# Gated linear attention: layout of the exponentials, one scaling per head, mask copies and square sums on ScalarE

## The chip, the core and the metric

The kernel runs on one core of one Trainium2 chip. The core has a matrix engine (PE, TensorE, with PEld for its weight loads), a vector engine (DVE, VectorE), a scalar engine (ACT, ScalarE), a general engine (POOL, GpSimd), and a queue engine (SP) from which this kernel sends all its DMA transfers. Each engine takes its instructions in order; they wait for each other through semaphores. Matrix products are written to PSUM, in banks of 128 partitions by 512 float32 numbers; everything else lies in SBUF, 128 partitions wide, and the large arrays in device memory (DRAM).

The metric is the device time of one execution in microseconds (us); lower is better. A profiled execution also has a span, the time from its first to its last instruction.

## The reference

One encoder layer is applied to two sequences of 512 tokens of width 1024. In order: a half-step SwiGLU network and a layer norm, an input projection, two groups of heads side by side (gated linear attention and grouped-query attention), an output projection and a layer norm, a second SwiGLU network and a layer norm, and a gated embedding. All is float32. The part that the change touches is the gated linear attention, four heads with keys of 64 and values of 128, in chunks of 64 tokens and in both directions:

```python
def gla_direction(q, k, v, log_a, inclusive):
    ...
    cum = jnp.cumsum(log_a.reshape(bsz, nc, c, h, dk), axis=2)
    mid = cum[:, :, c // 2 - 1:c // 2]
    last = cum[:, :, c - 1:]
    scores = jnp.einsum('bnihd,bnjhd->bnhij', q * jnp.exp(cum - mid), k * jnp.exp(mid - cum))
    mask = jnp.tril(jnp.ones((c, c), dtype=bool), 0 if inclusive else -1)
    scores = jnp.where(mask, scores, 0.0)
    o_intra = jnp.einsum('bnhij,bnjhe->bnihe', scores, v)
    upd = jnp.einsum('bnjhd,bnjhe->bnhde', k * jnp.exp(last - cum), v)
    ...
    o_inter = jnp.einsum('bnihd,bnhde->bnihe', q * jnp.exp(cum), states)
    return (o_intra + o_inter).reshape(bsz, n, h, dv)
```

The forward direction includes the token itself, the backward one does not. Their sum goes through an RMS norm per head and a gate.

## The kernel before

The whole layer is one program, unrolled. PE's order is written by hand: generators yield a few matrix products at a time, and a `Ticker` weaves the pieces of side work into the main stream of products. The order on the other engines and on SP is made by the framework from program order, dependences and its own time model when the program is built. Buffers come from pools with a fixed number of slots per tag; a tile whose slot is still in use makes its first writer wait for the last reader of the tile before it. PSUM has two pools of four banks: `pm` for the main projections, `pd` for the side work.

`Middle.gla(s)` is the gated linear attention of sequence s. It works on pairs of heads, two pairs for each of the two sequences, so four pairs run one after the other, woven into the products of the output projection (`wout`, products on L715, sums on L1107 and L1109, weights loaded on L149 and split into two parts on L137 and L138). The parts of `gla`:

- `pre(hp)` prepares a pair. L984 loads the log decays `l` (two directions) and L986 loads q and k of both heads of the pair, 128 partitions being two heads of 64, into the other half of the same tile. For each direction `dr` and each half `hf` of the tokens, L998 makes cumulative sums with a constant matrix (four products: a step), L1000 writes two exponentials of them, exp(+) for q and exp(-) for k, into E, and L1002 copies the chunk ends. There are four steps in a pair. L1009, L1011 and L1014 form the decay factors R between chunks. L1016 multiplies q and k by the exponentials into z. In z the two directions of one head lie on partitions 0 to 63 and 64 to 127, whereas in `l`, q, k and E the two heads do. So L1016 goes by direction, head and q or k: eight products of 64 partitions by 512 in a pair. The instructions on L1000 and L1014 are recorded under L176, the line of the helper `expln`.
- `one(h)` loads values gv and gates G of a head (L1024, L1025), transposes k (L1030, copied by L1032), forms the chunk updates (L1037), runs the state recurrence over the eight chunks in both directions (started by the copies L1044 and L1045, then 12 instructions on L1047 and L1049), scales the states (L1050, L1051), forms the scores of both directions (L1059), and writes them through a predicated copy per direction into A (L1061), which was set to zero once (L980).
- `two_a(h)` multiplies scores and states with values and queries into one bank o (L1070, L1073), squares it (L1076), sums the squares (L1078), and scales by norm and gate (L1081). `two_b(h)` transposes that (L1088) and splits it for the output projection (L1089, L1090).

The order around a pair is `one` of both heads, `two_a` of both heads, `pre` of the next pair, and so on. The tiles of `pre`, the states W and the attention's tile PT share one tag with three slots (`m8`). The first pair begins while grouped-query attention (`attn`, with L909 to L952) does its last pieces.

Of the kernel before, what the change touches and what calls it, by code (L numbers as in the profile page):

```python
# [12 lines left out]
AF = mybir.ActivationFunctionType  # L13
ALU = mybir.AluOpType
AX = mybir.AxisListType
# [5 lines left out]
NT = 4  # L21
# [14 lines left out]
            A=(157, 159, 160),  # L36
            seg=((2, 132), (2, 142), (18, 160), (18, 170), (43, 193), (43, 216), (178, 334)),
            b=(4, 3),
# [684 lines left out]
class Middle:  # L723
# [246 lines left out]
    def gla(self, s):  # L970
        nc, L = self.nc, self.L
        f, bw = slice(0, 64), slice(64, 128)
        T = {}

        def pre(hp):
            if hp == 0:
                T["mx"] = L.xp.tile([128, 4, 2, 512], F32R, tag="x", name="mixG")
                self.mix[s, 0] = T["mx"]
                T["A"] = self.vp.tile([128, 2, NT, 128], F32, tag="v", name="A")
                nc.gpsimd.memset(T["A"], 0.0)  # L980
            lq = self.m8("lq", (128, 2, 2, 512))
            l, qk = lq[:, 0].rearrange("p d (t c) -> p d t c", t=NT), lq[:, 1]
            for t in range(NT):
                nc.sync.dma_start(l[:, :, t], self.spill["l", s][t].rearrange("p (d c) -> p d c", d=2)[:, :, hp * 128:(hp + 1) * 128])  # L984
            for i in range(2):
                nc.sync.dma_start(qk[:, i], self.spill["gqk", s][2 * i + hp])  # L986
            yield
            R = [self.sp.tile([128, 8], F32, tag=f"R{e}", name=f"R{e}", bufs=2) for e in range(2)]
            E = self.m8("E", (128, 2, 2, 512))
            z = self.m8("qk1", (128, 2, 2, 512))  # L990
            for e in range(2):
                T["z", 2 * hp + e], T["R", 2 * hp + e] = z[:, e], R[e]
            for dr in range(2):
                sc = self.sp.tile([128, 2, 8], F32, tag="sc", name="sc")
                for hf in range(2):
                    b = L.bank_d().rearrange("p (a n) -> p a n", a=2)
                    for a in range(2):
                        nc.tensor.matmul(b[:, a, :132], l[:, dr, 2 * hf + a], self.L.U[:, dr], start=True, stop=True)  # L998
                    for j, sg in ((0, 1.0), (1, -1.0)):
                        L.expln(E[:, dr, j, hf * 256:(hf + 1) * 256].rearrange("p (a n) -> p a n", a=2),  # L1000
                                             b[:, :, :128], AF.Exp, scale=sg)
                    nc.vector.tensor_copy(  # L1002
                        sc[:, :, hf * 4:hf * 4 + 4].rearrange("p k (a c) -> p a k c", a=2),
                        b[:, :, 128:132].rearrange("p a (k c) -> p a k c", k=2))
                    if hf == 0:
                        yield
                ex = self.sp.tile([128, 7], F32, tag="ex", name="ex")
                if dr == 0:
                    nc.vector.tensor_tensor(ex, sc[:, 1, 0:7], sc[:, 0, 1:8], ALU.add)  # L1009
                else:  # L1010
                    nc.vector.tensor_tensor(ex, sc[:, 1, 1:8], sc[:, 0, 0:7], ALU.add)  # L1011
                for e in range(2):
                    rs, rd = slice(64 * e, 64 * e + 64), slice(64 * dr, 64 * dr + 64)
                    L.expln(R[e][rd, 1 - dr:8 - dr], ex[rs], AF.Exp)  # L1014
                    for i in range(2):
                        nc.vector.tensor_tensor(z[rd, e, i], qk[rs, i], E[rs, dr, i], ALU.mult)  # L1016
                yield

        def one(h):
            cs = slice(h * 128, (h + 1) * 128)  # L1020
            gv = self.m2("gvh", shape=(128, NT, 128))
            G = self.m2("Gh", shape=(128, NT, 128))
            for t in range(NT):
                nc.sync.dma_start(gv[:, t], self.spill["gv", s][t][:, cs])  # L1024
                nc.sync.dma_start(G[:, t], self.spill["G", s][t][:, cs])  # L1025
            q1, k1 = T["z", h][:, 0], T["z", h][:, 1]
            R = T["R", h]
            b = L.bank_d()
            for t in range(NT):
                nc.tensor.transpose(b[:, t * 128:(t + 1) * 128], k1[:, t * 128:(t + 1) * 128], L.ident)  # L1030
            kT = self.m2("kT", shape=(128, NT, 128))
            nc.scalar.activation(kT.rearrange("p a n -> p (a n)"), b, AF.Copy)  # L1032
            yield
            U = [L.bank_d().rearrange("p (c n) -> p c n", c=4) for _ in range(2)]
            for c in range(8):
                rw = slice(64 * (c % 2), 64 * (c % 2) + 64)
                nc.tensor.matmul(U[c % 2][:, c // 2], kT[rw, c // 2], gv[rw, c // 2], start=True, stop=True)  # L1037
            if h % 2 == 0:
                T["W"] = self.m8("W", (128, 2, 8, 128))
            W = T["W"][:, h % 2]  # L1040
            nc.gpsimd.memset(W[f, 0], 0.0)
            nc.gpsimd.memset(W[bw, 7], 0.0)
            up = lambda c, rd: U[c % 2][rd, c // 2]
            nc.scalar.activation(W[f, 1], up(0, f), AF.Copy)  # L1044
            nc.scalar.activation(W[bw, 6], up(7, bw), AF.Copy)  # L1045
            for c in range(1, 7):
                nc.vector.scalar_tensor_tensor(W[f, c + 1], W[f, c], R[f, c:c + 1], up(c, f), ALU.mult, ALU.add)  # L1047
                cb = 7 - c
                nc.vector.scalar_tensor_tensor(W[bw, cb - 1], W[bw, cb], R[bw, cb:cb + 1], up(cb, bw), ALU.mult, ALU.add)  # L1049
            nc.gpsimd.tensor_tensor(W[f, 1:8], W[f, 1:8], R[f, 1:8].unsqueeze(2).to_broadcast([64, 7, 128]), ALU.mult)  # L1050
            nc.gpsimd.tensor_tensor(W[bw, 0:7], W[bw, 0:7], R[bw, 0:7].unsqueeze(2).to_broadcast([64, 7, 128]), ALU.mult)  # L1051
            yield
            A = T["A"][:, h % 2]
            S = [L.bank_d().rearrange("p (a n) -> p a n", a=NT) for _ in range(2)]
            for t in range(NT):
                ts = slice(t * 128, (t + 1) * 128)
                for dr in range(2):
                    rd = slice(64 * dr, 64 * dr + 64)
                    nc.tensor.matmul(S[dr][:, t], k1[rd, ts], q1[rd, ts], start=True, stop=True)  # L1059
            for dr in range(2):  # L1060
                nc.vector.copy_predicated(A, self.L.mask[:, dr].unsqueeze(1).to_broadcast([128, NT, 128]), S[dr])  # L1061
            T["h", h] = gv, G, W, A
            yield

        def two_a(h):
            gv, G, W, A = T["h", h]
            q1 = T["z", h][:, 0]
            o = L.bank_d().rearrange("p (a n) -> p a n", a=4)
            for t in range(NT):
                nc.tensor.matmul(o[:, t], A[:, t], gv[:, t], start=True, stop=False)  # L1070
                for cc in range(2):
                    c = 2 * t + cc
                    nc.tensor.matmul(o[64 * cc:64 * cc + 64, t], q1[:, c * 64:(c + 1) * 64], W[:, c],  # L1073
                                     start=False, stop=True)
            sq = self.m2("osq", shape=(128, NT, 128))
            nc.scalar.activation(sq, o, AF.Square)  # L1076
            ss = L.small(NT, "oss")
            nc.vector.tensor_reduce(ss, sq, AX.X, ALU.add)  # L1078
            r = self.rms(ss, NT, 128.0, GN_EPS, "gn")
            for t in range(NT):  # L1080
                nc.vector.scalar_tensor_tensor(G[:, t], o[:, t], r[:, t:t + 1], G[:, t], ALU.mult, ALU.mult)  # L1081
            yield

        def two_b(h):
            G, mx = T["h", h][1], T["mx"]
            b = L.bank_d()
            for t in range(NT):
                nc.tensor.transpose(b[:, t * 128:(t + 1) * 128], G[:, t], L.ident)  # L1088
            nc.scalar.activation(mx[:, h, 0], b, AF.Identity, scale=self.L.gn)  # L1089
            nc.vector.scalar_tensor_tensor(mx[:, h, 1], b, self.L.gn, mx[:, h, 0].bitcast(F32), ALU.mult, ALU.subtract)  # L1090
            yield

        return pre, one, two_a, two_b

    def wout(self, s, part):
# [348 lines left out]
```

## Time and profile before

| | us |
|---|---|
| Three timed executions | 1960.98, 1953.67, 1956.47 |
| Their median | 1956.47 |
| Profiled execution, device time | 1953.48 |
| Its span | 1951.7 |
| PE busy in it | 1877.6 |
| DVE busy | 1413.1 |
| ACT busy | 873.8 |
| POOL busy | 860.5 |

The granted clock of PE over the span is 0.985 of full speed. Busy times of PE are modelled, since its products overlap. The profile names an instruction by line, engine and operation, then output and input tiles (in its naming `qk` and `qk1` stand for z, `pd` and `pm` for banks), then shapes as partitions by elements. An "x" gives a count. A bracket at the end of a line of the timeline is the time that the engine stood idle before the instruction, and what ended it. A line of who waited for whom gives the total in us, how often, and the longest. In the list of groups, the numbers behind the first bar are busy us in total and mean ns of one, those behind the second the idle us before them. A row of the stretches gives its length and then busy us and number of instructions of PE, PEld, DVE, ACT and POOL, the granted clock, the DMA engines' busy share and GB/s.

### The profile page before, as it was taken

To read this page: it belongs to the slowest core of one execution; us is meant where nothing else is said; L and a number is where in the kernel's file an instruction comes from. 1 tells how busy PE (TensorE), PEld (TensorE's weight loads), DVE (VectorE), ACT (ScalarE), POOL (GpSimd) and SP (SyncE) were. 2 spreads that over 40 slices of the span, in tenths; PEclk is the share of its full clock that TensorE was granted. 3 is DMA by queue.
4 is the path that set the end of the run, shared out by engine and by line. 5 is a ranking of instruction groups with operands and counts; after the bars stand their busy time and mean duration, and the time that the engine had idled before them with its cause. 6 is when DMAs were issued, how large, how long until landed. Compare 5 with 4: busy or idle time off the path is not lost. (4 is left out here: it accounts for less than half of the span.)

```text
span 1951.7 us, 25305 instructions
## 1 busy us (share of the span) xinstructions
PE 1877.6 (96%) x8838; PEld 1535.1 (79%) x8838; DVE 1413.1 (72%) x2143; ACT 873.8 (45%) x1654; POOL 860.5 (44%) x644
## 2 busy tenths in 40 slices
PE   7999999999999898989998898999999999999999
PEld 5788888888888777777876667888888888888787
DVE  7856566666886985788777879556566659895973
ACT  5445544444231355757752437445444442231342
POOL 0665565561550362342233343665565552451243
PEclk9999999999999998999998998999999999999999
DMA  4425443478865224222443231434443479766232
GB/s 180 162 103 173 169 150 144 158 279 343 316 252 195 91 72 156 84 82 92 140 152 87 87 119 55 161 114 158 173 161 141 162 274 338 297 256 247 76 122 84
DMA packets 104959, 322.22 MB, mean 165 GB/s; under 512 B 11008, under 2 KB 38400, under 8 KB 99456
## 3 DMA queue, kind: packets, MB, share of 16 engines
q1 hardware_dynamic: 104832, 320.61, 45.7%
q8 instruction: 70, 1.15, 0.2%
q14 instruction: 57, 0.47, 0.1%
HBM read 218.85 MB, written 101.71 MB: 164 GB/s over the span
## 5 line engine op out<-in xcount | busy, mean ns | idle before, releaser
L138 POOL TENSOR_TENSOR w<-raw,w 128x512 fp32r<-128x512 f32 (+1 forms) x318 | 431.8, 1367 | 750.3 <-ACT w L137 685.6
L137 ACT ACTIVATE w<-raw 128x512 fp32r<-128x512 f32 (+1 forms) x586 | 363.4, 624 | 449.2 <-POOL raw L269 85.8
L269 POOL TENSOR_TENSOR raw<-raw 128x512 f32<-128x512 f32 x240 | 355.9, 1491 | 227.4 <-DVE w L138 155.6
L425 PE MATMUL pm<-X,w 128*128 128x512 f32 x1848 | 434.6, 393 | 10.9 <-ACT X L137 7.8
L425 PEld LDWEIGHTS pm<-X,w 128*128 128x128 f32 x1848 | 347.2, 188 | 89.7 <-ACT X L137 8.6
L138 DVE TENSOR_TENSOR w<-raw,w 128x512 fp32r<-128x512 f32 x268 | 263.2, 990 | 115.5 <-ACT w L137 111.6
L425 PE MATMUL pd<-X,w 128*128 128x512 f32 x1320 | 307.9, 391 | 2.9 <-DVE w L138 2.2
L425 PEld LDWEIGHTS pd<-X,w 128*128 128x128 f32 x1320 | 247.5, 188 | 57.8 <-DVE w L138 3.0
L539 PE MATMUL pm<-w,XB 128*128 128x512 f32 x864 | 198.4, 389 | 0.8 <-DVE Y L523 0.8
L715 PE MATMUL pm<-w,h1T 128*128 128x512 f32 (+1 forms) x768 | 185.6, 384 | 14.0 <-ACT gr L757 9.9
L539 PEld LDWEIGHTS pm<-w,XB 128*128 128x128 f32 x864 | 162.0, 188 | 35.2 <-DVE Y L523 1.7
L138 DVE TENSOR_TENSOR hs<-sg,hs 128x512 fp32r<-128x512 f32 (+1 forms) x182 | 145.4, 818 | 49.6 <-ACT hs L137 48.4
L137 ACT ACTIVATE hs<-sg 128x512 fp32r<-128x512 f32 (+1 forms) x182 | 98.4, 561 | 166.1 <-DVE sg L391 64.8
L715 PEld LDWEIGHTS pm<-w,h1T 128*128 128x128 f32 x768 | 136.3, 195 | 36.5 <-ACT gr L757 10.1
L539 PE MATMUL pd<-w,XB 128*128 128x512 f32 x648 | 148.8, 389 | 0.0
L539 PEld LDWEIGHTS pd<-w,XB 128*128 128x128 f32 x648 | 121.6, 188 | 25.2
L523 DVE TENSOR_TENSOR Y<-Y,pm 128x512 f32<-128x512 f32 x104 | 70.4, 682 | 36.1 <-PE pm L539 36.0
L371 DVE TENSOR_TENSOR sg<-u,pm 128x512 f32<-128x512 f32 x22 | 15.1, 687 | 107.7 <-PE pm L425 107.7
L715 PE MATMUL pm<-w,h3T 128*128 128x512 f32 x384 | 90.6, 393 | 0.0
L715 PEld LDWEIGHTS pm<-w,h3T 128*128 128x128 f32 x384 | 71.2, 188 | 14.7 <-DVE h3T L670 0.2
L660 ACT ACTIVATE pd<-pd,c_lnT 128x512 f32<-128x512 f32 x48 | 36.0, 751 | 92.6 <-PE pd L658 92.6
L523 DVE TENSOR_TENSOR Y<-Y,pd 128x512 f32<-128x512 f32 x88 | 58.7, 678 | 19.3 <-PE pd L539 19.3
(237 smaller groups left out, 2542.1 us busy)
## 6 DMA issues: line engine op xcount, KB each, us to landing
hs<-hs SPq DMA_DIRECT2D x126, 512.0 KB, 2.6
XB<-hs SPq DMA_DIRECT2D x42, 1536.0 KB, 7.0
raw<-in_wgu SPq DMA_DIRECT2D x88, 512.0 KB, 3.4
raw<-in_wd SPq DMA_DIRECT2D x36, 512.0 KB, 7.2
hs_t<-hs SPq DMA_DIRECT2D x56, 256.0 KB, 2.5
XB<-hs_t SPq DMA_DIRECT2D x26, 512.0 KB, 5.1
raw<-in_wout SPq DMA_DIRECT2D x16, 512.0 KB, 3.6
raw<-in_wpg SPq DMA_DIRECT2D x16, 512.0 KB, 3.5
```

The costliest lines, as they stand in the source:

```text
L137: first = nc.scalar.activation(hi, raw, AF.Copy)
L138: (eng or nc.vector).tensor_tensor(lo, raw, hi.bitcast(F32), ALU.subtract)
L269: (sums or self.nc.gpsimd).tensor_tensor(o(), x(), y(), ALU.subtract)
L371: add = lambda o, x, y: nc.vector.tensor_tensor(o, x, y, ALU.add)
L425: nc.tensor.matmul(bank, w[:, a, kt * 128:(kt + 1) * 128], X[k][:, kt, b], start=(k in (0, 1, 4) and kt == 0 and m == 0), stop=(kt == 3 an ...
L523: nc.vector.tensor_tensor(yv, yv, bank, ALU.add)
L539: nc.tensor.matmul(b[t], h[:, a, t * 128:(t + 1) * 128], d[:, c], start=(k in (0, 4, 1) and g == 0 and x == 0), stop=(g == len(H) - 1 and ...
L660: nc.scalar.activation(p, p, AF.Identity, scale=self.lnT[:, c:c + 1], bias=self.lnT[:, c + 8:c + 9])
L715: nc.tensor.matmul(banks[t][:, :width], x[:, i, t * 128:(t + 1) * 128], w[a][:, j], start=(q == 0 and a == 0 and m == 0), stop=(q == nq - ...
```

## The change

Four things change, all in `gla`.

- q and k are no longer loaded beside `l`. Each is loaded twice, straight into z, once for the partitions of each direction: four transfers to 64 partitions in place of two to 128. z's tile is the target, so these loads come after z has its slot.
- The exponentials are written in the layout of z: for each step and each head separately, with 64 partitions, so four in a step in place of two.
- The scaling is one product for a head, over both directions, q and k (128 partitions by 1024), in place, once the second direction's exponentials are there: two in a pair in place of eight.
- In `one`, the predicated copy of the backward direction's scores is replaced by two copies on ACT of the diagonal 64 by 64 blocks, whole; the predicated copy of the forward direction then overwrites what the mask of L1061 selects. In `two_a`, the square over a bank and the sum on DVE are replaced by four squares on ACT, one for each 128 tokens, that give the sum as an accumulator output.

```diff
-            lq = self.m8("lq", (128, 2, 2, 512))
-            l, qk = lq[:, 0].rearrange("p d (t c) -> p d t c", t=NT), lq[:, 1]
+            l = self.m8("l", (128, 2, 2, 512))[:, 0].rearrange("p d (t c) -> p d t c", t=NT)
...
-            for i in range(2):
-                nc.sync.dma_start(qk[:, i], self.spill["gqk", s][2 * i + hp])
             yield
...
             z = self.m8("qk1", (128, 2, 2, 512))
+            for i in range(2):
+                src = self.spill["gqk", s][2 * i + hp].rearrange("(e p) c -> p e c", e=2)
+                for rd in (f, bw):
+                    nc.sync.dma_start(z[rd, :, i], src)
...
-                    for j, sg in ((0, 1.0), (1, -1.0)):
-                        L.expln(E[:, dr, j, hf * 256:(hf + 1) * 256].rearrange("p (a n) -> p a n", a=2),
-                                             b[:, :, :128], AF.Exp, scale=sg)
+                    for e in range(2):
+                        for j, sg in ((0, 1.0), (1, -1.0)):
+                            L.expln(E[64 * dr:64 * dr + 64, e, j, hf * 256:(hf + 1) * 256].rearrange("p (a n) -> p a n", a=2),
+                                    b[64 * e:64 * e + 64, :, :128], AF.Exp, scale=sg)
...
-                    for i in range(2):
-                        nc.vector.tensor_tensor(z[rd, e, i], qk[rs, i], E[rs, dr, i], ALU.mult)
+                    if dr == 1:
+                        nc.vector.tensor_tensor(z[:, e], z[:, e], E[:, e], ALU.mult)
...
-            for dr in range(2):
-                nc.vector.copy_predicated(A, self.L.mask[:, dr].unsqueeze(1).to_broadcast([128, NT, 128]), S[dr])
+            for r in (f, bw):
+                nc.scalar.activation(A[r, :, r], S[1][r, :, r], AF.Copy)
+            nc.vector.copy_predicated(A, self.L.mask[:, 0].unsqueeze(1).to_broadcast([128, NT, 128]), S[0])
...
-            nc.scalar.activation(sq, o, AF.Square)
             ss = L.small(NT, "oss")
-            nc.vector.tensor_reduce(ss, sq, AX.X, ALU.add)
+            for t in range(NT):
+                nc.scalar.activation(sq[:, t], o[:, t], AF.Square, accum_out=ss[:, t:t + 1])
```

## The prediction

> **What bounds the kernel now.** I read the page first, then the chain that ended last over 640 to 1200 us, then the stretch in which the changed lines run, by engine, then who waited for whom in it, then PE, DVE, ACT and SP in order of time. The profiled execution took 1953.48 us, of which the span is 1951.7 us; the median of the three timed runs is 1956.47 us, 3.0 us above it. The sum below is made against 1953.48 and put on the median at the end.
>
> ```profile
> span 1951.7 us, 25305 instructions
> ...
> 997.00:1152.00 155.00, 136.38 (x869) 100.52 (x868) 122.48 (x289) 52.35 (x135) 62.06 (x56) 0.94 0.36 109
> ```
>
> The second row is the stretch of the changed lines, a twelfth of the span; its busy columns are PE, PEld, DVE, ACT, POOL, then the granted clock. PE is busy 136.4 of 155 us. So whatever the change saves on DVE (122.5 us busy, the fullest engine but PE), no more than the 18.6 us in which PE stands still can be won, unless the clock changes.
>
> Gated linear attention runs there in four pairs of heads (two sequences, two pairs each). Within a pair PE goes: four steps of L998 (decay sums), other projections (L715), L1030 of the first head, then heads one and two, then L1070/L1073 of both. Who makes PE wait:
>
> ```profile
> PE pd L1030 <- DVE W L1047: 7.5, 4, 3.1
> ...
> PE pd L1070 <- DVE W L1047: 4.7, 4, 1.3
> ...
> 1012.68 0.63 PE L1030 MATMUL pd<-c_ident,qk 128*128 128x128 f32 x4 [1.02 <-DVE qk L1016]
> ...
> 1045.93 0.63 PE L1030 MATMUL pd<-c_ident,qk 128*128 128x128 f32 x4 [1.62 <-DVE qk L1016]
> ...
> 1083.49 0.63 PE L1030 MATMUL pd<-c_ident,qk 128*128 128x128 f32 x4 [1.04 <-DVE qk L1016]
> ...
> 1117.54 0.63 PE L1030 MATMUL pd<-c_ident,qk 128*128 128x128 f32 x4 [1.79 <-DVE qk L1016]
> ```
>
> The first two rows are the state recurrence (L1047/L1049), which the change leaves alone: 12.2 us that stay. The four timed rows are the first L1030 of each pair, waiting for the scaled q and k of L1016; the number in brackets is PE's wait, 1.02 + 1.62 + 1.04 + 1.79 = 5.47 us. This is the wait that the change addresses. Its start minus its wait is when PE was free: 1011.66, 1044.31, 1082.45, 1115.75.
>
> **The change part by part.** Durations first:
>
> ```profile
> L1016 DVE TENSOR_TENSOR qk<-lq,E 64x512 f32<-64x512 f32 x32 | 25.1, 806 | 0.4
> ...
> L1061 DVE COPY_PREDICATED A<-c_mask,pd 128x512 f32<-128x512 uint32 x16 | 11.6, 726 | 0.4
> ...
> L176 ACT ACTIVATE E<-pd 128x256 f32<-128x256 f32 x32 | 10.7, 375 | 6.1 <-PE pd L998 6.1
> ...
> L1078 DVE TENSOR_REDUCE oss<-osq 128x4 f32<-128x512 f32 x8 | 5.5, 684 | 11.3 <-ACT osq L1076 11.3
> ...
> L1076 ACT ACTIVATE osq<-pd 128x512 f32<-128x512 f32 x8 | 4.8, 598 | 36.3 <-PE pd L1073 36.3
> ...
> L1044 ACT ACTIVATE W<-pd 64x128 f32<-64x128 f32 x8 | 2.2, 270 | 11.2 <-PE pd L1037 11.2
> ...
> L942 ACT ACTIVATE o<-pd 64x256 f32<-64x256 f32 x3 | 1.1, 377 | 1.4 <-PE pd L939 1.4
> ...
> L176 ACT ACTIVATION_READ_ACCUMULATOR P<-pd,nm 128x1 f32 x2 | 0.4, 197 | 0.0
> ...
> L138 DVE TENSOR_TENSOR X<-rest,X 128x1024 fp32r<-128x1024 f32 x6 | 7.3, 1219 | 1.4 <-ACT X L137 1.4
> ```
>
> Scaling: 32 products of 64x512 (25.1 us) become 8 of 128x1024; the nearest row of that size is the last, 1.22 us, so 9.8 us: DVE loses 15.3 us. Exponentials: 32 of 128x256 become 64 of 64x256; a 64x256 read from PSUM takes 377 ns (L942), no less than 128x256, so ACT gains 32 x 0.377 = 12.1 us. Mask: 8 of 16 predicated copies go (5.8 us of DVE), 16 ACT copies of 64 x 4 x 64, 256 elements, come (6.0 us). Square sums: 8 reductions go (5.5 us of DVE); 8 squares of 128x512 become 32 of 128x128 with an accumulator read each. No row shows such a square; L1044 has its 128 elements, so 0.27 + 0.20 = 0.47 us each, 15.0 less 4.8: ACT gains 10.2 us. In sum DVE falls from 122 to about 96 us of the stretch, ACT rises from 52 to about 81. Neither number is the gain: the gain is what leaves PE's waits.
>
> **Step A, first L1030.** What must now be done before it is all four steps of exponentials, then one product of 128x1024. The last exponentials before:
>
> ```profile
> 1007.72 0.63 ACT L176 ACTIVATE E<-pd 128x256 f32<-128x256 f32 x2
> ...
> 1039.54 0.66 ACT L176 ACTIVATE E<-pd 128x256 f32<-128x256 f32 x2 [0.48 <-PE pd L998]
> ...
> 1041.46 0.36 ACT L176 ACTIVATE E<-pd 128x256 f32<-128x256 f32 x1
> ...
> 1079.27 0.63 ACT L176 ACTIVATE E<-pd 128x256 f32<-128x256 f32 x2
> ...
> 1112.94 0.63 ACT L176 ACTIVATE E<-pd 128x256 f32<-128x256 f32 x2
> ```
>
> They end at 1008.35, 1041.82, 1079.90 and 1113.57. Two take 0.66 us, so one more adds 0.28 and a step is 0.56 longer. The first two steps stand apart, with ACT waiting for PE between; the additions of the last two remain, 1.1 us (bounds 0.6 and 2.2). With the product of 1.22 and 0.05 us of handover, k is ready 2.4 us after these ends: 1010.7, 1044.2, 1082.3, 1115.9. PE is free at 1011.66, 1044.31, 1082.45, 1115.75. So PE itself becomes the last to come, and 5.3 of the 5.47 us go. The dependent rest of the pair (L1037, recurrence, second L1030, L1070) moves up with it. What queues behind: on DVE, behind the product that waits for the last exponential, its twin for the second head, then L1090 and L1107 or L1109, which PE needs only a bank or a projection later; on ACT, behind each longer step, weight splits (L137), made up to four pieces ahead, 0.56 us later each. With 2.2 for the additions, 1.1 us later in each pair, some 3.6 us of the 5.3 come back.
>
> **Step B, the recurrence's start.** DVE begins L1047 when ACT's L1045 is done and DVE's queue is clear:
>
> ```profile
> 1048.74 0.27 ACT L1045 ACTIVATE W<-pd 64x128 f32<-64x128 f32 x1
> ...
> 1049.56 0.33 DVE L1047 SCALAR_TENSOR_TENSOR W<-W,R,pd 64x128 f32<-64x128 f32 x1
> ...
> 1120.35 0.27 ACT L1045 ACTIVATE W<-pd 64x128 f32<-64x128 f32 x1
> ...
> 1121.86 0.34 DVE L1047 SCALAR_TENSOR_TENSOR W<-W,R,pd 64x128 f32<-64x128 f32 x1
> ```
>
> DVE was late by 0.55 us in pair 2 and 1.24 in pair 4. Pair 2's goes, as DVE has its products done a microsecond earlier. In pair 4 other work (L1109, L1090, L509) queues on DVE behind the products and moves up less than L1045 does: I count 0.5 of 1.24 (bounds 0 and 1.24). Step B gives 1.0 us.
>
> **Step C, masks and squares.** L1070 waits for the recurrence (row above), not for the masked scores, so the copies hide behind the recurrence, 12 instructions of 0.33 us and more a head; without that cover they would cost two copies and a handover, 0.8 us a head. Four squares in a row take about 4 x 0.39 us (they overlap by 0.1 or less) against 0.60 + 0.69 now: 0.2 us later. That shows only at the last head, where PE has nothing else to put in front: -0.2 us.
>
> **Step D, the loads.** q and k are now loaded twice, four loads of 256 KB for two, into z itself, so they wait for z's buffer; SP sends in order.
>
> ```profile
> 1002.69 1.10 PE L939 MATMUL pd<-PT,V 128*128 128x256 f32 x8
> ...
> 1014.00 1.16 PE L1037 MATMUL pd<-gvh,kT 64*128 64x128 f32 x16
> ...
> L1024 SPq DMA_DIRECT2D gvh<-sp_gv x32: 319/430/1089, 1001.5 to 1116.2; - x32
> ...
> DMA to landing us min/median/max: 1.7/2.3/7.1
> ...
> L986 SPq DMA_DIRECT2D lq<-sp_gqk x8: 430/514/598, 999.9 to 1091.8; - x8
> ...
> DMA to landing us min/median/max: 3.0/4.0/4.5
> ...
> 1034.05 0.44 PE L1073 MATMUL pd<-W,qk 128*64 128x128 f32 x4
> ...
> 1038.81 0.33 SPq L149 DMA_DIRECT2D raw<-in_wout  x1
> ...
> 1072.18 0.44 PE L1073 MATMUL pd<-W,qk 128*64 128x128 f32 x4
> ...
> 1082.63 0.33 SPq L149 DMA_DIRECT2D raw<-in_wout  x1
> ...
> 1105.49 0.44 PE L1073 MATMUL pd<-W,qk 128*64 128x128 f32 x4
> ...
> 1112.58 0.33 SPq L149 DMA_DIRECT2D raw<-in_wout  x1
> ```
>
> z's buffer comes free when the last reader before it ends: for pair 1 attention's last values (L939, 1003.8), for the others the pair before's last L1073 (1034.5, 1072.6, 1105.9). Four issues of 0.51 and a landing of 3.0 to 4.5 us later make 5.0 to 6.5: 1008.8 to 1010.3, 1039.5 to 1041, 1077.6 to 1079.1, 1110.9 to 1112.4. The exponentials now end at about 1009.5, 1042.9, 1081.0 and 1114.7, so the loads hide, by nothing in pair 1 and by 2 us in the others. Behind them on SP wait the heads' gv and G (L1024, L1025) and weights (L149). In pair 1, the tightest, eight issues of 0.43 us behind z's last (1005.9) end at 1009.3 and land 2.3 us later, 1011.6; L1037, which needs them, follows L1030 by 1.3 us and comes at 1013 at the earliest. I take 0; late by a microsecond, pair 1 loses one.
>
> A rule speaks against this step. The Trainium skill, "SBUF — State Buffer", Door 1, says that 64 partitions reach only 8 of the 16 DMA ports, so a transfer to 64 runs at half rate. By its 27.2 GB/s a port the megabyte would take an estimated 4.8 us instead of 2.4, so that the last load lands 2.4 us later than above, 2.4 us too late in pair 1 and 0.4 in the others; the sum would be about 2.6 us. No load of the rows above goes to 64 partitions, so the trace cannot say.
>
> Sum: 5.3 + 1.0 - 0.2 = **6.1 us**, 1953.5 to 1947.4; on the median 1950.4. What follows the stretch, the output projection, is led by PE and moves up whole.
>
> **The rivals.** (1) *The clock.* After some waits PE runs slowly:
>
> ```profile
> 1064.00:1073.00 9.00, 9.00 (x45) 5.69 (x46) 3.99 (x12) 1.34 (x4) 3.37 (x3) 0.62 0.41 118
> 1126.00:1133.00 7.00, 6.28 (x33) 4.63 (x35) 4.61 (x11) 1.14 (x3) 3.35 (x2) 0.54 0.00 0
> ```
>
> Granted 0.62 of 9 us and 0.54 of 7 us, they lose 3.4 + 3.2 = 6.6 us. Shorter waits could spare both: 6.1 + 6.6 = 12.7, so 1944. For it: the second stretch begins at the longest wait, 3.1 us. Against it: most of that wait is recurrence and stays, and the first begins after a wait of 1.3 only. The Trainium skill, "TensorE: Matmul & The Clock Gate", Part 1, lets the clock fall after an idle window of about 3.4 us that runs free of the kernel; by that rule the first stretch would not be there, so the trace agrees in part.
>
> (2) *SP's order*, the slower side. If z's loads come to stand behind the next weight load (L149 at 1038.81, 1082.63, 1112.58, each held by its own wait), q and k land 0.33 + 2.05 + 4.5 us later, and L1030 follows 1.3 us after: 1047.0, 1090.8 and 1120.8 for 1045.9, 1083.5 and 1117.5, so 1.1 + 7.3 + 3.3 = 11.7 us slower: 1968. It decides from a landing after about 1044.7, 1082.2 and 1116.2. For it: SP's order is made anew when the program is built. Against: in the code z's loads stand ahead of the heads' loads, and SP is idle at 1072.6 and 1106.
>
> (3) *ACT takes DVE's place.* If copies, weight splits (L137) and squares get in between the exponentials, the additions are 2.2 us, step B goes, and about 1.5 us are left: 1955. For it: ACT's 29 us more. Against: ACT is a third busy here.
>
> That the change does not do what it says is no case: the instructions follow from the code.
>
> **How the numbers follow.** Forecast 0.45; clock 0.20; ACT 0.22; SP 0.13. The likeliest gives 1950. The clock case with the runs' spread reaches down to 1942, the ACT case and an SP case with one late pair up to 1961; the rest of SP's is left out. About 0.5%, 10 us, can be told from no change here. Faster by more: most of the clock case and a little of the forecast, 0.23. Slower by more: most of SP's, 0.11. Between: 0.66.
>
> **What would show it.** Right: first L1030 of each pair with no wait for L1016's successor, 8 products of about 1.22 us, L1047/L1049 waits as before, ACT near 81 us of the stretch. Wrong: L1030 or the product waiting for a DMA (step D), for an exponential (step A), L1070 for an ACT copy (step C), or the two slow-clock stretches gone or new ones elsewhere.

## The result, and the profile after

The changed kernel takes 1939.28 us (median of four executions, 1938.49 to 1939.72). The kernel before, run beside it, has a median of 1955.07 (four executions, 1949.62 to 1960.98). The ratio of the two is 0.9929 with a 95% interval of 0.9903 to 0.9956, so by the ratio some 14 us or 0.7% are gained. The prediction was 1950.0 with a range of 1942 to 1961: too little gain, and outside the range by 2.7 us.

The profiled execution of the changed kernel took 1939.51 us (span 1937.7), 13.97 less than the one before. All of it lies in the stage of the changed lines. I take that stage from the first decay sum of pair 1 to the last transposes of the last head (L1088 before, L1091 after); those are the bounds of the row of the stretches. First the kernel before:

```profile
1001.31:1148.59 147.28, 128.66 (x827) 94.34 (x827) 116.38 (x275) 48.03 (x126) 59.24 (x53) 0.94 0.35 104
```

The same stage after:

```profile
1002.05:1134.85 132.80, 122.64 (x828) 91.35 (x827) 94.29 (x233) 68.17 (x230) 59.13 (x53) 0.99 0.49 131
```

The stage is 14.5 us shorter. PE does the same work (827 and 828 products). Its busy time falls by 6.0 us, as its granted clock rises from 0.94 to 0.99, and its idle time, length less busy, falls by 8.5 us (18.6 to 10.2). DVE falls by 22 us and ACT rises by 20. So there are two terms of similar size, waits and clock, and the prediction had counted 6 us of the one and none of the other.

Where the waits went: PE's rows of who waited for whom after, over the same stretch as the rows shown in the prediction (total, times, longest):

```profile
PE pd L1039 <- ACT kT L1034: 3.8, 4, 2.1
PE pd L1076 <- POOL W L1053: 3.3, 4, 1.1
PE pd L1032 <- ACT mixG L1092: 0.9, 1, 0.9
PE pd L1039 <- ACT w L137: 0.8, 1, 0.8
PE pd L1091 <- DVE Gh L1084: 0.6, 1, 0.6
```

Not only has the wait for the scaled q and k gone, as foreseen. No row is left in which PE waits for the recurrence (L1049 and L1051 after), where before 12.2 us stood in two rows. How that came about can be read in pair 2. Before, DVE (end of the first head's recurrence, then the mask copies), then PE:

```profile
1053.34 0.34 DVE L1047 SCALAR_TENSOR_TENSOR W<-W,R,pd 64x128 f32<-64x128 f32 x1
1053.71 0.35 DVE L1049 SCALAR_TENSOR_TENSOR W<-W,R,pd 64x128 f32<-64x128 f32 x1
...
1054.70 0.73 DVE L1061 COPY_PREDICATED A<-c_mask,pd 128x512 f32<-128x512 uint32 x1
...
1055.91 0.72 DVE L1061 COPY_PREDICATED A<-c_mask,pd 128x512 f32<-128x512 uint32 x1
```

```profile
1053.83 0.99 PE L1030 MATMUL pd<-c_ident,qk 128*128 128x128 f32 x4 [1.82 <-DVE W L1047]
```

The second head's transposes start 0.15 us after the last L1047 (1053.34 + 0.34 = 1053.68). But they read none of its results: they take k of the *other* head. What they take from it, on this reading, is a bank. The pool `pd` has four, and one head takes five: the transposes, the two update banks `U`, the two score banks `S`. Both score banks are held until DVE's mask copies, which queue behind the recurrence, so the earliest bank is the update bank that the last L1047 reads. The wait at L1070 reads the same way. PE in pair 2, before:

```profile
1062.72 0.46 PE L1070 MATMUL pd<-gvh,A 128*128 128x128 f32 x2 [1.35 <-DVE W L1047]
```

This is the first head's product. Its masked scores A were done at 1056.63 (1055.91 + 0.72), and it still waits for the second head's recurrence: it writes a new bank, and only there do the two meet. After, in the place of the second head's transposes, ACT, then PE, then DVE:

```profile
1051.53 0.77 ACT L1063 ACTIVATE A<-pd 64x256 f32<-64x256 f32 x2 [2.16 <-PE pd L1061]
```

```profile
1052.35 0.66 PE L1032 MATMUL pd<-c_ident,qk 128*128 128x128 f32 x4
```

```profile
1053.19 0.34 DVE L1049 SCALAR_TENSOR_TENSOR W<-W,R,pd 64x128 f32<-64x128 f32 x1
1053.56 0.35 DVE L1051 SCALAR_TENSOR_TENSOR W<-W,R,pd 64x128 f32<-64x128 f32 x1
```

ACT is done with the backward scores at 1052.30, and PE's transposes follow at 1052.35 with no wait. DVE ends the first head's recurrence at 1053.91: the transposes now run beside it. That is a reading of times, since the trace writes every bank as `pd`; the experiments had to show whether it is the bank.

### The profile page after: what moved, and what is told of

Its sections match the earlier page's. It is cut to its first block, busy times and chain, and to the rows that moved or that the text cites. A ratio compares the mean times of both kernels' runs of the same rounds, so it can differ in the third digit from the quotient of the medians.

```text
span 1937.7 us, 25351 instructions
## 1 busy us (share of the span) xinstructions
PE 1872.4 (97%) x8838; PEld 1533.4 (79%) x8838; DVE 1391.2 (72%) x2103; ACT 894.0 (46%) x1758; POOL 863.1 (45%) x644
```

## The experiments

All were timed in five rounds against the kernel before on the same chip, whose median was 1954.27 us (29 executions), 1953.76 (23) and 1955.96 (23) in the three sets. The theory at the start was the bank; its rivals were DVE's load (22 us less work on the fullest engine but PE), the earlier scaling, and the clock.

### The parts one by one

`m_only`: before, with the mask copies alone changed.

```diff
-            for dr in range(2):
-                nc.vector.copy_predicated(A, self.L.mask[:, dr].unsqueeze(1).to_broadcast([128, NT, 128]), S[dr])
+            for r in (f, bw):
+                nc.scalar.activation(A[r, :, r], S[1][r, :, r], AF.Copy)
+            nc.vector.copy_predicated(A, self.L.mask[:, 0].unsqueeze(1).to_broadcast([128, NT, 128]), S[0])
```

> The kernel before with the mask edit alone. Bank theory (the second head's transposes and the first product with A waited for a PSUM bank, not for the recurrence's result, and the ACT copies of the backward scores free one early): the waits for the recurrence before the second transposes (7.5 us) and before the first L1070 (4.7 us) fall below 2 us each, the waits of the first transposes for the scaling stay near 5.5 us; 7 to 12 us faster. DVE-load theory (the gain follows the work taken off DVE): 5.8 of the 26.6 us are taken off, so about 3 us faster, the waits for the recurrence stay at 12 us. Step as forecast: no change.

`s_only`: before, with the loads into z, the exponentials in the new layout and one scaling per head, that is, the first three points of the change. `q_only`: before, with the four squares that give their sums. `no_m`: the changed kernel with the mask copies put back, which is the diff of `m_only` undone.

> The kernel before with the loads, exponentials and scaling edits alone. Bank theory: the waits of the first transposes shrink from 5.5 to under 2 us, the 12 us of waits for the recurrence stay; 3 to 6 us faster. DVE-load theory: 15.3 of 26.6 us taken off DVE, about 8 us faster.

> The kernel before with the square sums alone on ACT. Bank theory: no wait changes, within 2 us of before. DVE-load theory: 5.5 of 26.6 us taken off, about 3 us faster.

> The changed kernel with both predicated copies on DVE put back. Bank theory: the 12 us of waits for the recurrence come back; 3 to 6 us faster than before, 8 to 11 us slower than the changed kernel. DVE-load theory: 20.8 of 26.6 us are still off DVE, about 11 us faster than before.

| | median us | range, executions | ratio, 95% interval |
|---|---|---|---|
| m_only | 1941.62 | 1939.26 to 1943.47, 6 | 0.9940 (0.9928 to 0.9952) |
| s_only | 1953.66 | 1946.54 to 1961.07, 12 | 1.0007 (0.9989 to 1.0025) |
| q_only | 1947.93 | 1945.99 to 1959.41, 12 | 0.9986 (0.9969 to 1.0002) |
| no_m | 1956.83 | 1951.10 to 1960.52, 12 | 1.0009 (0.9995 to 1.0023) |

By the ratios the mask copies alone bring 12 of the 14 us. In `m_only` the two rows of waits for the recurrence are gone, but for 1.2 us at L1037, and those for the scaling stay. PE's rows of who waited for whom, then its stage:

```profile
PE pd L1030 <- DVE qk L1016: 5.7, 4, 1.8
PE pd L1074 <- POOL W L1051: 2.2, 3, 0.8
PE pd L1037 <- DVE W L1047: 1.2, 1, 1.2
```

```profile
1002.43:1136.53 134.10, 123.62 (x828) 91.94 (x826) 111.86 (x267) 53.97 (x142) 58.75 (x53) 0.99 0.38 114
```

Everything else without them (`no_m`) brings nothing, though it contains the step that I had priced at 5.3 us. The bank theory foresaw the first, but also expected some microseconds to be left in `s_only` and `no_m`; there it missed. Why can be read in `no_m`, first in PE's rows of who waited for whom:

```profile
PE pd L1032 <- DVE W L1049: 7.1, 4, 2.2
PE pd L1072 <- DVE W L1049: 4.9, 4, 1.3
PE pd L1039 <- ACT kT L1034: 3.0, 3, 2.1
```

and then in its stage, among the stretches:

```profile
1003.17:1154.12 150.95, 134.17 (x828) 97.71 (x826) 98.09 (x241) 62.13 (x214) 59.15 (x53) 0.90 0.43 115
```

The first L1032 of a pair no longer waits for the scaling, but 3.0 us come back one step later at L1039, the bank waits are there again (12.0 us), and the granted clock falls to 0.90, below that of before. So it is over all executions: the median clock of the span is 0.982 in `no_m` and 0.986 in the kernel before beside it. What the earlier scaling gains may be lost there again. The theory of DVE's load fails here: in `no_m` DVE is busy for 98.1 us, nearly as little as after, and the time is that of before; in `m_only` it is busy for 111.9 us, and the gain is there.

### The bank, without the work

`hold`: the changed kernel, with one more read of the bank that ACT frees, a single column, on DVE behind the predicated copy. It costs DVE 0.13 us a head; ACT's copies stay as they are.

```diff
             nc.vector.copy_predicated(A, self.L.mask[:, 0].unsqueeze(1).to_broadcast([128, NT, 128]), S[0])
+            late = self.sp.tile([128, 1], F32, tag="late", name="late")
+            nc.vector.tensor_copy(late, S[1][:, 0, 0:1])
```

`no_s`: before, with mask copies and squares changed but not the loads, exponentials and scaling. `m_dve`: the changed kernel with the same diagonal copies on DVE in place of ACT:

```diff
-                nc.scalar.activation(A[r, :, r], S[1][r, :, r], AF.Copy)
+                nc.vector.tensor_copy(A[r, :, r], S[1][r, :, r])
```

> The changed kernel, with one more read of the backward scores on DVE, one column of 128 partitions, behind the predicated copy, which itself stands behind the recurrence. The copies on ACT and all work taken off DVE stay; only the bank is held until then, for 0.16 us more of DVE a head. Bank theory: the waits for the recurrence before the second transposes and before the first product with A come back, 8 to 11 us slower than the changed kernel. DVE-load theory: 1.3 us of DVE in all, within 2 us of the changed kernel.

> The changed kernel with the two copies of the diagonal blocks as plain copies on DVE in place of ACT. They stand in DVE's queue behind the recurrence. Bank theory: like the one with both predicated copies, 8 to 11 us slower than the changed kernel. DVE-load theory: two copies of about 0.4 us a head, 6 us of DVE back, about 3 us slower than the changed kernel.

> The kernel before with mask and square sums on ACT, loads, exponentials and scaling as before. Bank theory: like the mask edit alone, 7 to 12 us faster than before, with the first transposes' waits for the scaling near 5.5 us. DVE-load theory: 11.3 of 26.6 us taken off, about 6 us faster.

`hold` took 1956.71 us (12 executions, ratio 1.0010, 0.9992 to 1.0027), `m_dve` 1956.09 (12, 1.0010, 0.9994 to 1.0027), `no_s` 1941.43 (6, 0.9937, 0.9915 to 0.9959). One column read late on an otherwise complete change takes back the whole gain. In `hold`'s pair 2, ACT is done with the scores as early as in the changed kernel, measured from them, and PE waits all the same, until the recurrence has read its last update:

```profile
1056.07 0.77 ACT L1063 ACTIVATE A<-pd 64x256 f32<-64x256 f32 x2 [2.13 <-PE pd L1061]
```

```profile
1057.77 0.34 DVE L1049 SCALAR_TENSOR_TENSOR W<-W,R,pd 64x128 f32<-64x128 f32 x1
...
1059.75 0.13 DVE L1066 COPY late<-pd 128x1 f32<-128x1 f32 x1
```

```profile
1058.25 0.63 PE L1032 MATMUL pd<-c_ident,qk 128*128 128x128 f32 x4 [1.36 <-DVE W L1049]
```

ACT ends at 1056.84, the late read comes at 1059.75, the last L1049 ends at 1058.11, and PE starts at 1058.25. The copies and DVE's lighter load are as in the changed kernel, and only the bank is held. So the wait is for a bank, and when it comes free depends on the place of its last reader in an engine's queue. `hold` was expected to keep a few microseconds of the scaling, as `no_m` was; it keeps none either, with the clock of its stage at 0.91.

### The clock by itself

What was still mixed was the clock. In the profiled executions so far it is low in the stage wherever the waits for a bank are, so a gain in waits and one in clock came together, with one exception. That is `q_only`, whose profiled execution is one of its faster ones (1947.77 us). Its waits for a bank are those of before, and its clock is not (first PE's rows of who waited for whom, then the stretch that the prediction shows of before with a clock of 0.94):

```profile
PE pd L1030 <- DVE W L1047: 6.8, 4, 3.1
PE pd L1070 <- DVE W L1047: 5.3, 4, 1.3
```

```profile
997.00:1152.00 155.00, 136.50 (x892) 101.45 (x891) 122.42 (x292) 57.80 (x194) 64.01 (x57) 0.99 0.36 110
```

So these waits do not cost clock in every execution, and without a loss of clock they are worth some 6 us: `m_only` took 1941.34 in its profiled execution, at 0.99 too (though without the change to the squares). The scatter also says why the median of `q_only` can be 6 us below that of before while its ratio is not clear of 1: its executions lie between 1945.99 and 1959.41, as widely as those of before. Whether the squares make the faster ones more frequent is not shown.

`fill` pulls the two apart by an edit: before, with each score product issued twice, the second time over the same numbers. The score products of a head then take 2.16 us in place of 1.16, so PE does 1.0 us more work a head, all of it ahead of the wait for a bank (the expectation had put it at 1.09). Nothing can start earlier; only the idle time shrinks. `no_m_fill` is the same in `no_m`.

```diff
-                    nc.tensor.matmul(S[dr][:, t], k1[rd, ts], q1[rd, ts], start=True, stop=True)
+                    for _ in range(2):
+                        nc.tensor.matmul(S[dr][:, t], k1[rd, ts], q1[rd, ts], start=True, stop=True)
```

> Before, with each of L1059's score products issued twice (the second overwrites the first with the same numbers): 16 more PE products a head, 1.09 us of PE work, all ahead of a wait of 1.3 to 3.1 us for a bank, which therefore shrinks by 1.09 us while no bank comes free earlier and nothing after it can start earlier. If the slow-clock stretches are set off by those waits (clock theory), the executions lose their upper half: median 1946 to 1950, highest below 1956, and the granted clock of the stage rises from 0.94 to about 0.98. If the waits alone cost time and the clock's loss is not tied to them, the median stays at 1953 to 1957 with the scatter of before (1946 to 1961).

> The same doubling in no_m (after with both predicated copies on DVE, 1956.8 us). Clock theory: what no_m gains at the first L1032 comes to light once the bank waits are filled, so that it falls to 1945 to 1950. Bank theory without the clock: it stays at 1955 to 1958.

`fill` took 1948.64 us (1945.71 to 1951.69, 12 executions; ratio 0.9970, 0.9953 to 0.9987), `no_m_fill` 1947.67 (1944.57 to 1950.18, 12; 0.9966, 0.9952 to 0.9980). With 8 x 1.0 = 8 us of useless work added, the kernel is 6 us (by the ratio) to 7 us (by the medians) faster, and `no_m` with it 8 to 9 (measured in another set than `no_m` itself). The stage of `fill`:

```profile
1002.88:1144.40 141.52, 131.85 (x955) 99.41 (x954) 117.34 (x275) 47.84 (x126) 58.68 (x53) 0.99 0.37 108
```

It has 127 products more than before and is 5.8 us shorter, at a clock of 0.99 against 0.94. The bank waits of `fill`, in PE's rows of who waited for whom:

```profile
PE pd L1030 <- DVE W L1047: 2.0, 4, 0.9
PE pd L1071 <- DVE W L1047: 0.8, 3, 0.3
```

Before they were 7.5 and 4.7 us, with a longest of 3.1; here no single one is over 0.9. The scatter agrees. Beside `fill`, the executions of the kernel before go from 1946.28 us (mean clock of the span 0.989) to 1960.24 (0.984), and 17 of the 23 are longer than the longest of `fill`; those of `fill` stay within 6 us, at 0.988 and 0.989. So, on this reading, the clock takes next to nothing from some executions of the kernel before and up to some 14 us from others, and what fills the waits takes it back.

### What is late next

In the changed kernel PE's next wait that a small edit can reach is for POOL, which scales the states of the second head (L1053). `w_act`: the changed kernel with the backward states of the second head scaled on ACT, chunk by chunk. It was run twice, the second time beside the changed kernel itself (`after_b`).

```diff
-            nc.gpsimd.tensor_tensor(W[bw, 0:7], W[bw, 0:7], R[bw, 0:7].unsqueeze(2).to_broadcast([64, 7, 128]), ALU.mult)
+            if h % 2 == 0:
+                nc.gpsimd.tensor_tensor(W[bw, 0:7], W[bw, 0:7], R[bw, 0:7].unsqueeze(2).to_broadcast([64, 7, 128]), ALU.mult)
+            else:
+                for c in reversed(range(7)):
+                    nc.scalar.activation(W[bw, c], W[bw, c], AF.Identity, scale=R[bw, c:c + 1])
```

> The changed kernel with the backward states of the second head of each pair scaled chunk by chunk on ACT in place of POOL. In the changed kernel PE waits for POOL's second scaling before the second head's products with the states, 0.75 to 1.07 us in each pair, 3.3 us in all. If that wait is what is now late: it goes, 2 to 3 us faster than the changed kernel. If something else comes at the same time (PE's queue, the squares): within 1 us of it.

> The changed kernel again, for a comparison with the two others of this call on one chip: 1938 to 1941 us by every theory.

> After with the second head's backward states scaled on ACT in place of POOL, beside after itself. If POOL's scaling (3.3 us of PE waits at the second head's products with the states) is what is late next, it is 1 to 3 us faster than after; if another wait takes its place, it is within 0.5 us.

`w_act` took 1938.20 us (6 executions) and, as `w_act_b`, 1939.44 (6), `after_b` 1940.10 (6, 1937.00 to 1942.76). The ratios against before in that last set are 0.9926 (0.9903 to 0.9949) for `w_act_b` and 0.9927 (0.9902 to 0.9952) for `after_b`: no difference. PE's rows of who waited for whom in `w_act_b` say why:

```profile
PE pd L1039 <- ACT kT L1034: 3.8, 4, 2.1
PE pd L1077 <- ACT A L1067: 2.6, 4, 0.9
```

The wait for POOL, 3.3 us, is replaced by one of 2.6 us for the mask copies on ACT, which now stand behind the scalings in ACT's queue. No version beats the changed kernel by an amount that these runs can tell.

## Why the prediction was wrong

**What bounds the kernel: the step that failed.** The prediction read PE's two largest waits as "the state recurrence (L1047/L1049), which the change leaves alone: 12.2 us that stay". The recurrence does stay: 12 instructions a head, and its rows look alike before and after. What was wrong is the reading of the row. "PE pd L1030 <- DVE W L1047" names the instruction that released PE, and I took that for a result that PE needed. L1030 of the second head needs nothing of it: its operands are `c_ident` and `qk`, and the row itself says so. The same row should have led to the pool: four banks, five tiles a head, and two of them held by the mask copies that the change moves. In the changed kernel the 12.2 us are gone, and 3.3 us of waiting for POOL stand in their place; `m_only` shows that the mask copies do it, and `hold` that it is the bank.

**Step C**, accordingly, had the sign and the size wrong: "-0.2 us" for masks and squares, for the reason that L1070 waits for the recurrence and not for the masked scores. It is the step that carries the change: 12 us with the mask copies alone. For the squares the price was fair: `q_only` is 0.9986 with an interval that includes 1. Four squares with their reads take 1.1 us in a row (the first two are shown at the end), less than the 1.56 estimated.

**Step A** was right in its place and wrong in what it is worth. The wait of 5.47 us for the scaling is gone, with 1.4 us left for other releasers (0.9 in the L1032 row shown, 0.3 and 0.2 in smaller ones). The products of 128x1024 take 1.22 us when nothing disturbs them, as priced. But what is late next was not seen: kT, the copy of the transposes on ACT. In pair 1 it is held up from DVE. I named what queues there behind the second head's product as L1090 and L1107; in this pair L1013 does too, the sum for the decay factors, which ACT needs before it comes to kT. DVE, ACT and POOL in pair 1 of the changed kernel:

```profile
1010.65 1.23 DVE L1018 TENSOR_TENSOR qk<-qk,E 128x1024 f32<-128x1024 f32 x1 [0.50 <-ACT E L176]
1011.79 0.16 DVE L1004 COPY sc<-pd 128x8 f32<-128x8 f32 x1
1011.87 1.22 DVE L1018 TENSOR_TENSOR qk<-qk,E 128x1024 f32<-128x1024 f32 x1
1013.00 1.23 DVE L1013 TENSOR_TENSOR ex<-sc 128x7 f32<-128x7 f32 x1
```

```profile
1014.26 0.42 ACT L176 ACTIVATE R<-ex 64x7 f32<-64x7 f32 x2 [1.79 <-DVE ex L1013]
1014.71 0.60 ACT L1034 ACTIVATE kT<-pd 128x512 f32<-128x512 f32 x1
```

```profile
1012.08 3.35 POOL L138 TENSOR_TENSOR w<-raw,w 128x512 fp32r<-128x512 f32 x2 [3.22 <-issue]
```

L1013 is a sum of seven columns; it comes last and takes 1.23 us, beside two sums on POOL. So ACT stands idle for 1.79 us until 1014.26, kT is copied at 1014.71, and PE waits for it, 2.07 us as the longest in its row. The other waits are 0.4 to 0.8 us. In pairs 2 and 3 L1013 comes ahead of the products, in pair 4 between them, and ACT does other work first, in pair 2 four pieces for the output projection:

```profile
1044.32 0.42 ACT L176 ACTIVATE R<-ex 64x7 f32<-64x7 f32 x2 [0.43 <-DVE ex L1013]
1044.77 0.69 ACT L1092 ACTIVATE mixG<-pd,c_gn 128x512 fp32r<-128x512 f32 x1
1045.36 0.62 ACT L137 ACTIVATE w<-raw 128x512 fp32r<-128x512 f32 x1
...
1046.97 0.59 ACT L1034 ACTIVATE kT<-pd 128x512 f32<-128x512 f32 x1
```

Over the four pairs PE waits 3.8 us for kT, 3.0 of them at the first heads. So most of the 5.47 us moved on by one step. With the clock spared on both sides, `no_m_fill` against `fill` is 1947.67 to 1948.64, one microsecond, less than these runs can tell, for loads, exponentials, scaling and squares together. Between `m_only` and the changed kernel (1941.62; 1939.28 and 1940.10) it is some 2 us, and the intervals overlap. One sum was a little off: with the additions at 2.2 us, the step's own times give back 3.3 us, not 3.6.

**Step B** cannot be told apart in the totals; its 1.0 us is no more than what is left there.

**Step D** held. L1018 is never last to wait for a load (its group waits 0.5 us in all, for exponentials), so the loads hide. First the products' row among the groups of the stage, then the row of z's loads (issue in ns, then landing in us, each minimum, median, maximum), both of the changed kernel:

```profile
L1018 DVE TENSOR_TENSOR qk<-qk,E 128x1024 f32<-128x1024 f32 x8 | 10.7, 1358 | 0.5 <-ACT E L176 0.5
```

```profile
L991 SPq DMA_DIRECT2D qk<-sp_gqk x16: 597/605/611, 1000.8 to 1099.8; - x16
...
DMA to landing us min/median/max: 3.8/4.8/7.3
```

The issue takes 0.60 us where 0.51 was assumed, and the median landing 4.8 us against 4.0 before. The Trainium skill, "SBUF — State Buffer", Door 1, would have transfers to 64 partitions at half rate; the landing of a transfer a little later than before neither shows nor excludes that, as issue and queueing are in it, but nothing of it reached PE.

**Rivals.** The *clock* (0.20) came true as a mechanism and nearly in size: it had 6.6 us to spare, and `fill` is 5.8 us shorter in the stage and 7.3 in the median. The argument against it, that "most of that wait is recurrence and stays", was the same misreading. It went with the waits that Step C removes, not with those of Step A: in the profiled stages of `s_only` and `no_m` the clock was lower still, 0.86 and 0.90. *SP's order* (0.13) did not come. *ACT takes DVE's place* (0.22) describes part of the waits for kT, but not the change. The true case, bank and clock together, was not among the rivals: 6 to 7 us of clock (`fill` against before) and 6 to 7 us of bank waits (`m_only` against `fill`).

**What would show it.** For the signs that it named: "first L1030 of each pair with no wait for L1016's successor" and "8 products of about 1.22 us" came, but for one product of 2.30 us. "L1047/L1049 waits as before" did not, and "the two slow-clock stretches gone" did. ACT rose by 20 us of the stage, not by 28, and DVE fell by 22, not by 26.6.

## What to carry to other kernels

A row that says PE waits for an instruction names a release, which need not be a result that PE reads: compare the tile that was released with what the waiting instruction reads, and where they have nothing in common, count the buffers of the pool that it writes. Then ask which queue each reader of those buffers stands in, since one cheap read behind a long chain holds a bank as long as the chain does; moving that one read to an engine that is free was worth 12 us here, and 18 us less work on DVE without it nothing (`no_m`). Where waits of a microsecond or more recur, look at the granted clock behind them too, and fill them with work that does nothing to see how much of the loss is the clock's.

## What the runs showed of the hardware

The granted clock fell after short waits. In the profiled execution of the kernel before, the waits for a bank are 0.7 to 3.1 us, some 7 to 9 us apart within a pair, and the two slow stretches of the prediction begin behind one of 1.35 us (the L1070 row above) and one of 3.13. In `s_only`, whose waits for a bank are up to 2.2 us, the clock is 0.50 to 0.53 for ten microseconds and more at two places:

```profile
1030.00:1042.00 12.00, 12.00 (x50) 7.74 (x50) 5.01 (x14) 2.04 (x5) 2.41 (x2) 0.53 0.05 5
...
1104.00:1114.00 10.00, 10.00 (x38) 6.53 (x38) 3.33 (x11) 1.60 (x4) 0.29 (x1) 0.50 0.06 13
```

PE is busy throughout in both, but slow. It does not happen after each such wait nor in each execution (`q_only` has the waits at 0.99), and which condition sets it off was not settled; the changed kernel has such a stretch too, behind its 2.07 us wait:

```profile
1016.00:1021.00 5.00, 5.00 (x33) 3.75 (x30) 3.53 (x11) 1.99 (x5) 2.36 (x2) 0.66 0.72 210
```

The Trainium skill, "TensorE: Matmul & The Clock Gate", Part 1, has the clock halved after an idle window of about 3.4 us; the half agrees with 0.50, but no wait in these rows is that long, nor is the 3.13 of before, for which the prediction had let the rule pass. Nearer is the same page's section "A second HAM failure mode: psum-queue depth-cycling", by which, in a bfloat16 kernel there, short idles of PE between groups of products, in cycling through PSUM banks, set the clock swinging between half and full. `fill` agrees with that: without any bank free earlier, shorter idles alone kept all of its executions at 0.988 and 0.989.

The sum L1013 of 128x7 takes 0.17 us in three pairs and 1.23 in pair 1, beside POOL's two sums (rows above). The Trainium skill, "SBUF — State Buffer", section "SBUF: two separate sides", says that DVE instructions with two inputs from SBUF and POOL instructions that read SBUF share a port pair, which one holds for a whole instruction while the other stands. The rows agree, and in the three other pairs POOL runs no sum beside L1013; but no run took POOL's work away.

Squares of 128x128 with an accumulator read follow each other at 0.25 us on ACT, the read overlapping the next square, where I had put 0.39:

```profile
1030.77 0.28 ACT L1081 ACTIVATE osq<-pd 128x128 f32<-128x128 f32 x1 [3.80 <-PE pd L1076]
1030.94 0.20 ACT L1081 ACTIVATION_READ_ACCUMULATOR osq<-pd 128x1 f32 x1
1031.03 0.27 ACT L1081 ACTIVATE osq<-pd 128x128 f32<-128x128 f32 x1
```
